# The recurrence branch of a hybrid encoder layer: products that read PSUM, first taps on ScalarE, gates as plain float32

## The chip, the cores and the metric

The kernel runs on one NeuronCore of a Trainium2 chip. The core has five engines with a queue each: TensorE (PE; its weight loads appear as PEld), VectorE (DVE), ScalarE (ACT), GpSimd (POOL) and SyncE (SP), which here only issues DMAs. Matrix products are written to PSUM; everything else lies in SBUF. The metric is the device time of one execution in microseconds (us). Where a time comes from the trace, it is counted from the first instruction of the profiled execution.

## The reference

One layer of an encoder trunk is computed for 1024 tokens of width 1024 in float32: a mixer of two groups, a cross-attention into 256 memory rows, and a gated MLP with a small convolution. The change lies in group A of the mixer. Cut to that group:

```
h    = rms_norm(x, attn_norm)
proj = h @ w_in                       # 1024 x 1440
xr, yg = proj[..., :512], proj[..., 512:1024]
xf = depthwise_conv(xr, conv_w[0], conv_b[0], 3, 0)    # width 4, causal
xb = depthwise_conv(xr, conv_w[1], conv_b[1], 0, 3)    # width 4, anti-causal
def rg_lru(x, ...):
    r = sigmoid(block_diag(x, w_a) + b_a)              # 8 blocks of 64 x 64
    i = sigmoid(block_diag(x, w_i) + b_i)
    log_a = -8 * r * softplus(-lam);  a = exp(log_a)
    b = sqrt(-expm1(2 * log_a)) * (i * x)
    return scan of h[t] = a[t] * h[t-1] + b[t]         # backwards for xb
lru_out = (rg_lru(xf, ...) + rg_lru(xb, ...)) * gelu(yg)
```

The other 416 columns of `proj` are the latents of group B, an attention of 8 heads.

## The kernel before

Channels lie on the 128 partitions and the 1024 tokens along the free dimension, so the 512 channels of group A are four tiles j = 0..3 (`NJ`), each with two directions d. The normalised input stands transposed in SBUF as two halves: `hT[h][0]` is rounded to float32r, `hT[h][1]` is what the rounding left out. Every large product is made of three products of such halves (`mm3`, lines 110 to 113: high by high, high by low, low by high); weights are split into `whi` and `wlo` by `wsplit` (lines 124 to 142), mostly on POOL (lines 133 and 134).

`in_proj` (line 297) makes one 128 x 1024 tile of the projection with 2 x 8 x 3 products of 512 columns in a PSUM tile of pool `pb2`. That pool holds two such tiles, and both the projections and, later, the latents (`pslat`) and the stage behind them take turns in it.

`xr_stage` (line 340) copies the projection into SBUF on ACT (line 345), between three zero columns on either side (lines 343, 344). The copy frees the PSUM tile. `y_stage` (line 348) does the same for the GeLU branch (line 351) and then forms y * (1 + tanh(c * (y + 0.044715 y^3))) with three products on DVE (lines 353, 354, 356) around a tanh on ACT (line 355).

`lru_stage` (line 358) does the two directions of one tile. For each direction: the first tap with the bias on POOL (line 365), three more taps on DVE (line 367); the split of the result, `xh` on ACT (line 370) and `xl` on DVE (line 371); the gates as 4 x 3 products into four PSUM tiles `psg` of 512 columns (the call at line 379; every product is issued by the helper at line 108); tanh, exp, tanh and square root on ACT (lines 385 to 390, which switch between two activation tables, so that each direction loads a table twice); then on DVE `m` (line 392) and `thi` (line 393), on POOL their product (line 394), and on DVE the scan (lines 397, 399). The two directions are added on POOL (line 401), and line 403 multiplies the sum with the GeLU branch on DVE.

The gate weights of two tiles at a time come from `gate_unit` (line 314): eight DMAs into a zeroed staging tile `raw` (pool `wp`, two of them, shared with all weight loads), then split into `whi` and `wlo` (two of the twelve `w` tiles). In lines 508 to 525 the stages are called in this order: the first two projections and gate weights, the rotary tables, then for each tile its GeLU branch, its recurrence and the projection of a later tile; behind the last tile come the latents (line 417), eight of them, one for each 128 tokens. Behind those come the query, key and value products (`pq`, `pk`).

Instructions are not issued in the order of the program. The framework that builds the kernel orders each engine's queue beforehand, by the order of the program and by when it expects operands and buffers to be ready; it puts in all waits, also those for a buffer's release. On the chip each queue then runs in that fixed order. Tiles with one tag share its buffers: `xf` and `xr` have two each, `th0` two, `th1` four.

Of the kernel before, what the change touches and what calls it, by code (L numbers as in the profile page):

```python
# [11 lines left out]
F32 = mybir.dt.float32  # L12
# [7 lines left out]
S = 1024  # L20
# [63 lines left out]
def trunk_layer(ctx: ExitStack, tc: tile.TileContext, a: dict, out: bass.AP):  # L84
# [35 lines left out]
    def wunit(load, n=1024, gains=None, eng="pool"):  # L120
        raw = wload(load)
        return wsplit(raw, n, gains, eng)
# [34 lines left out]

# [1 line left out]
    bcs = ExitStack()  # L159
# [17 lines left out]

    # normed x, transposed
    hT = [[big.tile([P, KD, 512], F32R, tag="big", name=f"hT{h}{s}") for s in range(2)] for h in range(2)]
# [21 lines left out]

    # parameter columns
    RR = tp.tile([P, 6, P], F32, tag="xr", bufs=2, name="RR")
# [31 lines left out]
    def col(name, i=0):  # L235
        r = rows[name] + i
        return pcols[:, r:r + 1]
# [28 lines left out]

    # half biases, softplus of -lambda
    hb = const.tile([P, 16], F32, name="hb")
# [45 lines left out]
    def gate_unit(jj):  # L314
        def load(raw):
            pool.memset(raw, 0.0)
            rv = raw.rearrange("p (j d g c) -> p j d g c", j=2, d=2, g=2)
            for b in range(2):
                for gi, nm in enumerate(("lru_w_a", "lru_w_i")):
                    for d in range(2):  # L320
                        nc.sync.dma_start(
                            rv[64 * b:64 * b + 64, :, d, gi, 64 * b:64 * b + 64],
                            a[nm][0, d].rearrange("(j b) p c -> b p j c", b=2)[b][:, 2 * jj:2 * jj + 2, :])
        wg[jj] = wunit(load)

# [13 lines left out]

    def xr_stage(j):  # L340
        ps = in_proj(j * P)
        xr = tp.tile([P, S + 6], F32, tag="xr", bufs=2, name="xr")
        pool.memset(xr[:, 0:3], 0.0)
        pool.memset(xr[:, S + 3:S + 6], 0.0)
        act.activation(xr[:, 3:S + 3], ps, AF.Copy)
        return xr

    def y_stage(j):
        ps = in_proj(LRU + j * P)
        y = lru[:, j, :]  # L350
        act.activation(y, ps, AF.Copy)
        t = tp.tile([P, S], F32, tag="yt", bufs=1, name="yt")
        dve.scalar_tensor_tensor(t, y, 0.044715, y, ALU.mult, ALU.mult)
        dve.scalar_tensor_tensor(t, t, 1.0, y, ALU.add, ALU.mult)
        act.activation(t, t, AF.Tanh, scale=math.sqrt(2.0 / math.pi))
        dve.scalar_tensor_tensor(y, t, 1.0, y, ALU.add, ALU.mult)

    def lru_stage(j, xr):
        hs = []
        for d in range(2):  # L360
            i = d * 4 + j
            xf = tp.tile([P, S], F32, tag="xf", name="xf")
            cw = [col("conv_w", (d * 4 + k) * 4 + j) for k in range(4)]
            o = 3 * d
            pool.tensor_scalar(xf, xr[:, o:o + S], cw[0], col("conv_b", i), ALU.mult, ALU.add)
            for k in range(1, 4):
                dve.scalar_tensor_tensor(xf, xr[:, o + k:o + k + S], cw[k], xf, ALU.mult, ALU.add)
            xh = tp.tile([P, S], F32R, tag="th0", name="xh")
            xl = tp.tile([P, S], F32R, tag="th1", bufs=4, name="xl")
            act.activation(xh, xf, AF.Copy)  # L370
            dve.tensor_sub(xl, xf, f(xh))
            wh, wl = wg[j // 2]
            pss = []
            for h in range(2):
                for g in range(2):
                    ps = pb1.tile([P, 512], F32, tag="b1", name="psg")
                    wo = ((j % 2) * 4 + d * 2 + g) * P
                    sl = slice(h * 512, (h + 1) * 512)
                    mm3(ps, wh[:, wo:wo + P], wl[:, wo:wo + P], xh[:, sl], xl[:, sl], True, True)
                    pss.append(ps)  # L380
            thr = tp.tile([P, S], F32, tag="th0", name="thr")
            thi = tp.tile([P, S], F32, tag="th1", bufs=4, name="thi")
            for h in range(2):
                for g in range(2):
                    act.activation((thr, thi)[g][:, h * 512:(h + 1) * 512], pss[h * 2 + g], AF.Tanh,
                                   bias=hb[:, g * 8 + i:g * 8 + i + 1], scale=0.5)
            av = tp.tile([P, S], F32, tag="a", name="av")
            act.activation(av, thr, AF.Exp, bias=sp4[:, 8 + i:9 + i], scale=sp4[:, 8 + i:9 + i])
            act.activation(thr, thr, AF.Tanh, bias=sp2[:, i:i + 1], scale=sp2[:, i:i + 1])
            act.activation(thr, thr, AF.Sqrt, scale=0.25)  # L390
            m = thr
            dve.scalar_tensor_tensor(m, av, 1.0, thr, ALU.add, ALU.mult)
            dve.scalar_tensor_tensor(thi, thi, 1.0, xf, ALU.add, ALU.mult)
            pool.tensor_mul(thi, thi, m)
            h = thi
            if d == 0:
                dve.tensor_tensor_scan(h, av, thi, 0.0, ALU.mult, ALU.add)
            else:
                dve.tensor_tensor_scan(h[:, ::-1], av[:, ::-1], thi[:, ::-1], 0.0, ALU.mult, ALU.add)
            hs.append(h)  # L400
        pool.tensor_add(hs[0], hs[0], hs[1])
        y = lru[:, j, :]
        dve.scalar_tensor_tensor(y, hs[0], 0.5, y, ALU.mult, ALU.mult)

    # latents, q, k, v
    wl_ = []
# [29 lines left out]
    def rotated(dst, src, tmp, i, t0, n, nh):  # L436
        # dst [P, n, nh, 32]: the rows src of token tiles t0.., rotated, times their gains
        C = rC[i][:, t0:t0 + n, :].unsqueeze(2).to_broadcast([P, n, nh, ROPE])
        for a_, b_ in ((0, HALF), (HALF, 0)):
            Sb = rS[i][:, t0:t0 + n, a_:a_ + HALF].unsqueeze(2).to_broadcast([P, n, nh, HALF])  # L440
            pool.tensor_tensor(tmp[:, :, :, a_:a_ + HALF], src[:, :, :, b_:b_ + HALF], Sb, ALU.mult)
        pool.tensor_tensor(dst, src, C, ALU.mult)
        pool.tensor_add(dst, dst, tmp)
# [96 lines left out]
    def inv_root(r, tmp):  # L540
        # r -> r ** -0.5 by Newton steps from a guess out of the exponent
        y, b = tmp
        dve.tensor_scalar(y.bitcast(I32), r.bitcast(I32), 1, None, ALU.logical_shift_right)
        dve.tensor_scalar(y.bitcast(I32), y.bitcast(I32), -1, 0x5f3759df, ALU.mult, ALU.add)
        for k in range(3):
            dve.tensor_tensor(b, r, y, ALU.mult)
            dve.scalar_tensor_tensor(b, b, -0.5, y, ALU.mult, ALU.mult)
            dve.scalar_tensor_tensor(y if k < 2 else r, b, 1.5, y, ALU.add, ALU.mult)

    def head_stats(p, th, tmp):  # L550
        # rotates the queries of a head pair, token tiles th * 4 ..; sums of squares of its queries and keys
        if th == 0:
# [24 lines left out]
    def squares(key, src, first, acc, tmp, last=False):  # L577
        # running sum of squares over the channel tiles of a group
        if first:
            sacc[key] = acc([P, S], "acc")  # L580
            act.activation(sacc[key], src, AF.Square)
        else:
            t = tmp([P, S], "acct")
            act.activation(t, src, AF.Square)
            if last:
                dve.tensor_add(sacc[key], sacc[key], t)
                return
            for c in chunks():
                pool.tensor_add(sacc[key][:, c], sacc[key][:, c], t[:, c])
# [3 lines left out]

    # keys and values of the memory
    mT = [[wp.tile([P, 4, MEM], F32R, tag="w", name="mT") for _ in range(2)]
# [80 lines left out]

# [1 line left out]
    cs = ExitStack()  # L678
# [98 lines left out]
    def values(u, part):  # L777
        # part 0 / 1: the two halves of the keys of query pair u
        H, qq = divmod(u, NT // 2)
# [73 lines left out]

# [1 line left out]
    xp = ctx.enter_context(tc.tile_pool(name="xp", bufs=NT, side="right", reuse_waits="tile"))  # L855
# [48 lines left out]
    def turned(xs, dst, o):  # L904
        # xs [P, D] transposed into dst(q) = (hi, lo) [P, 4, ...] at columns o..
        for q in range(2):
# [10 lines left out]
    def headnorm(ps):  # L917
        # rms-norm of the heads of ps [P, 512], without gains
        s4 = dp.tile([P, MH], F32, tag="s4", bufs=2, name="s4")
# [196 lines left out]

# [1 line left out]
    fs = ExitStack()  # L1118
# [96 lines left out]
```

## Time and profile before

| what | value |
|---|---|
| device time, three runs | 1489.05, 1489.11, 1490.06 us (median 1489.11) |
| span of the profiled execution | 1487.0 us, 17902 instructions |
| the profiled execution's own time beside its span | not listed apart; the median of the runs lies 2.1 us above the span |
| PE busy | 1408.4 us (95%) |
| DVE, ACT, POOL busy | 905.4 (61%), 547.8 (37%), 631.1 us (42%) |
| PE busy in the 190 us from 40 to 230 | 152.4 us, at a mean granted clock of 0.89 |

The profile is one execution. "Busy" is the time in which an engine worked on an instruction; a row of the groups gives the line, engine, operation, the tiles written and read, the shapes, the count, then the sum and the mean (ns) of the durations and the idle time of the engine just before them. In the page's strip of 40 slices one slice is 37 us and each digit is a busy share in tenths. Matrix products overlap in their pipeline, so the durations of neighbouring products overlap, and their cost is read from one start to the next. A wait is put down to the engine whose signal came last.

The recurrence branch lies between 40 and 230 us. From 320 us on PE is busy 1146 of 1167 us.

### The profile page before, as it was taken

Reading aid. Unit: us, or ns where it says so; the run is one execution under the profiler, and the core shown is the slowest. Engines: PE = TensorE matmul, PEld = TensorE weight load, DVE = VectorE, ACT = ScalarE, POOL = GpSimd, SP = SyncE. Lnnn points to the kernel's source line nnn. Section 1 sums busy time; section 2 is a strip of 40 time slices with the busy share of each in tenths; the row PEclk is TensorE's granted clock in tenths of the full one; section 3 lists DMA queues with packets and bytes.
Section 4 is the critical chain, followed back from the end, with each engine's and each line's share of the span. In section 5 each row is a group of like instructions: output and inputs, shape, how many; then the busy total and the mean of one; then the engine's idle time right before and its main releaser. Section 6 shows DMA issues by size and latency. Waiting matters only on the chain.

```text
span 1487.0 us, 17902 instructions
## 1 busy us (share of the span) xinstructions
PE 1408.4 (95%) x6996; PEld 1186.8 (80%) x6996; DVE 905.4 (61%) x1260; ACT 547.8 (37%) x904; POOL 631.1 (42%) x612
## 2 busy tenths in 40 slices
PE   6888678998999999999999999999999999999998
PEld 5766578787889888888888888888888888888887
DVE  5879887799999855576645434435343444534335
ACT  5255674688888842355322110101111020111110
POOL 7768686456786811010334142322314232231310
PEclk9989889999999999999999999999999999999999
DMA  5211011200000052101112020211102021110102
GB/s 182 64 38 34 25 43 29 100 1 1 1 1 1 1 172 84 57 2 29 43 29 85 29 71 29 66 47 43 57 29 71 29 59 55 43 57 29 57 0 113
DMA packets 72036, 70.92 MB, mean 48 GB/s; under 512 B 4859, under 2 KB 59408, under 8 KB 71952
## 3 DMA queue, kind: packets, MB, share of 16 engines
q1 hardware_dynamic: 71951, 69.78, 15.1%
q8 instruction: 55, 0.90, 0.2%
q14 instruction: 30, 0.24, 0.1%
HBM read 65.58 MB, written 4.19 MB: 47 GB/s over the span
## 4 chain that ended last, share of the span: by engine, by line
PE 71%; DVE 8%; ACT 3%; POOL 2%; issue 1%; DMA 0%; ACTq 0%; DVEq 0%; POOLq 0%; SPq 0%
PE psup L108 32%; PE psdn L108 16%; PE psP L108 6%; PE psq L108 3%; PE psS L108 3%; PE psmo L108 3%; PE po L108 2%; DVE st L752 2%; DVE pT L775 2%; PE psT L771 2%; PE pq L108 1%; ACT pr L756 1%; PE psn L910 1%; PE psMS L108 1%; PE pmo L108 1%
## 5 line engine op out<-in xcount | busy, mean ns | idle before, releaser
L108 PE MATMUL psup<-h,whi 128*128 128x512 f32 x1408 | 437.5, 389 | 1.1 <-DVE gu L1143 0.9
L108 PEld LDWEIGHTS psup<-h,whi 128*128 128x128 f32 x1408 | 264.2, 188 | 56.8 <-issue 1.2
L133 POOL TENSOR_SCALAR whi<-raw 128x1024 fp32r<-128x1024 f32 (+2 forms) x82 | 91.1, 1111 | 447.3 <-PE psup L108 239.8
L108 PE MATMUL psup<-h,wlo 128*128 128x512 f32 x704 | 273.9, 389 | 0.0
L1142 DVE SCALAR_TENSOR_TENSOR gu<-psup,fcw,gu 128x1023 f32<-128x1023 f32 x44 | 56.4, 1283 | 251.3 <-ACT gu L1141 251.3
L1141 ACT ACTIVATE gu<-psup,fcw 128x1024 f32<-128x1024 f32 x44 | 53.2, 1209 | 421.9 <-PE psup L108 421.9
L134 POOL TENSOR_TENSOR wlo<-raw,whi 128x1024 fp32r<-128x1024 f32 (+2 forms) x82 | 203.2, 2478 | 6.2
L1172 DVE TENSOR_TENSOR x<-x,psdn 128x512 f32<-128x512 f32 x176 | 119.3, 685 | 104.0 <-PE psdn L108 103.3
L108 PEld LDWEIGHTS psup<-h,wlo 128*128 128x128 f32 x704 | 132.1, 188 | 27.4
L108 PE MATMUL psdn<-wlo,ah 128*128 128x512 f32 x336 | 130.7, 389 | 0.0
L108 PE MATMUL psdn<-whi,al 128*128 128x512 f32 x336 | 130.7, 389 | 0.0
L108 PE MATMUL psdn<-whi,ah 128*128 128x512 f32 x336 | 130.5, 389 | 0.1
L108 PE MATMUL psS<-kT,qT 96*128 96x512 f32 x384 | 103.9, 404 | 5.3 <-ACT pr L756 5.2
L758 POOL TENSOR_SCALAR pr<-pr,st 128x1024 f32<-128x1024 f32 x64 | 72.0, 1125 | 53.6 <-DVE st L757 32.1
L108 PE MATMUL psin<-hT,whi 128*128 128x512 f32 (+1 forms) x288 | 87.4, 386 | 1.1 <-ACT hT L199 1.0
L775 DVE TENSOR_TENSOR pT<-psT,pT 128x512 fp32r<-128x512 f32 x128 | 84.5, 679 | 6.2 <-ACT pT L774 6.1
L756 ACT ACTIVATE pr<-psS,st,rqk 128x1024 f32<-128x1024 f32 x64 | 77.2, 1207 | 18.2 <-DVE st L754 14.0
L108 PEld LDWEIGHTS psS<-kT,qT 96*128 96x128 f32 x384 | 67.5, 189 | 19.3 <-ACT pr L756 8.1
L752 DVE TENSOR_REDUCE st<-psS 128x1 f32<-128x1024 f32 x64 | 77.7, 1214 | 8.0 <-PE psS L108 8.0
L108 PE MATMUL po<-pT,vt 128*128 128x256 f32 x512 | 72.2, 287 | 3.6 <-DVE pT L775 3.3
L108 PEld LDWEIGHTS psdn<-whi,ah 128*128 128x128 f32 x336 | 63.1, 188 | 13.5 <-DVE x L1172 0.5
L771 PE MATMUL psT<-ident,pr 128*128 128x128 f32 x512 | 68.3, 273 | 5.7 <-POOL pr L758 3.7
(307 smaller groups left out, 2651.7 us busy)
## 6 DMA issues: line engine op xcount, KB each, us to landing
raw<-in_w_up SPq DMA_DIRECT2D x44, 512.0 KB
raw<-in_w_down SPq DMA_DIRECT2D x22, 512.0 KB
xt<-in_x SPq DMA_DIRECT2D x8, 512.0 KB
raw<-in_w_in SPq DMA_DIRECT2D x8, 512.0 KB
raw<-in_w_mem_kv SPq DMA_DIRECT2D x8, 512.0 KB
raw<-in_w_out SPq DMA_DIRECT2D x8, 512.0 KB
x<-in_x SPq DMA_DIRECT2D x8, 512.0 KB
out<-x SPq DMA_DIRECT2D x7, 512.0 KB
```

The source lines that it names most:

```text
L108: return pe.matmul(ps, lhsT=l, rhs=r, start=start, stop=stop)
L133: pool.tensor_scalar(hi[:, sl], raw[:, sl], 1.0, 0.0, ALU.mult, ALU.add)
L134: pool.tensor_sub(lo[:, sl], raw[:, sl], f(hi)[:, sl])
L752: dve.tensor_reduce(st[:, 0:1], psS, AX.X, ALU.max, negate=True)
L756: act.activation(pr, psS, AF.Exp, bias=st[:, 1:2], scale=r, accum_out=st[:, 2:3])
L758: scaled[s] = pool.tensor_scalar(pr, pr, st[:, 3:4], 0.0, ALU.mult, ALU.add)
L771: pe.transpose(ps[:, i * P:(i + 1) * P], pr[:, (n * 4 + i) * P:(n * 4 + i + 1) * P], ident)
L775: dve.tensor_sub(pTs[s // 2][n][1][:, :, qi * P:(qi + 1) * P], pv, f(dh))
L910: pe.transpose(ps[:, k * P:(k + 1) * P], xs[:, kk * P:(kk + 1) * P], ident)
L1141: act.activation(g, ps, AF.Identity, bias=fcv[:, 3, jj:jj + 1], scale=fcv[:, 1, jj:jj + 1])
L1142: dve.scalar_tensor_tensor(g[:, 1:], ps[:, :S - 1], fcv[:, 0, jj:jj + 1], g[:, 1:], ALU.mult, ALU.add)
L1172: dve.tensor_add(xs, xs, ps)
```

## The change

The change touches `gate_unit`, `xr_stage`, `y_stage` and `lru_stage`; elsewhere only comment lines are blanked.

- The projection of the x-branch is no longer copied to SBUF. Two Identity activations on ACT (one for each direction) read the PSUM tile and write the first tap with the bias; they write all 1024 columns, so no zero columns are needed. The six other taps, on DVE, read the projection in PSUM, and each leaves out the columns that would fall outside. The taps stand in `xr_stage`, thus ahead of the recurrence of the tiles before. Their two results use the tag `xf` for even tiles and `xr` for odd ones.
- The GeLU branch is not copied either. ACT squares it out of PSUM, and the two remaining DVE products read it there.
- The gates are one product of plain float32 operands in place of three of float32r halves: no `xh` and `xl`, no split of the gate weights, which are loaded into one `w` tile without a staging tile.
- The sum of the two directions moves from POOL to DVE, and so does the product of line 394 for the last tile.

```diff
     def gate_unit(jj):
-        def load(raw):
-            pool.memset(raw, 0.0)
-            rv = raw.rearrange("p (j d g c) -> p j d g c", j=2, d=2, g=2)
...
-        wg[jj] = wunit(load)
+
+        w = wp.tile([P, 1024], F32, tag="w", name="wgate")
+        pool.memset(w, 0.0)
+        rv = w.rearrange("p (j d g c) -> p j d g c", j=2, d=2, g=2)
...
+        wg[jj] = w
...
     def xr_stage(j):
+
         ps = in_proj(j * P)
-        xr = tp.tile([P, S + 6], F32, tag="xr", bufs=2, name="xr")
-        pool.memset(xr[:, 0:3], 0.0)
-        pool.memset(xr[:, S + 3:S + 6], 0.0)
-        act.activation(xr[:, 3:S + 3], ps, AF.Copy)
-        return xr
+        xfs = [tp.tile([P, S], F32, tag=("xf", "xr")[j % 2], bufs=2, name="xf") for _ in range(2)]
+        cw = [[col("conv_w", (d * 4 + k) * 4 + j) for k in range(4)] for d in range(2)]
+        for d in range(2):
+            act.activation(xfs[d], ps, AF.Identity, bias=col("conv_b", d * 4 + j), scale=cw[d][3 - 3 * d])
+        for n in range(1, 4):
+            dve.scalar_tensor_tensor(xfs[0][:, n:], ps[:, :S - n], cw[0][3 - n], xfs[0][:, n:], ALU.mult, ALU.add)
+        for n in range(1, 4):
+            dve.scalar_tensor_tensor(xfs[1][:, :S - n], ps[:, n:], cw[1][n], xfs[1][:, :S - n], ALU.mult, ALU.add)
+        return xfs
 
     def y_stage(j):
         ps = in_proj(LRU + j * P)
         y = lru[:, j, :]
-        act.activation(y, ps, AF.Copy)
         t = tp.tile([P, S], F32, tag="yt", bufs=1, name="yt")
-        dve.scalar_tensor_tensor(t, y, 0.044715, y, ALU.mult, ALU.mult)
-        dve.scalar_tensor_tensor(t, t, 1.0, y, ALU.add, ALU.mult)
+        act.activation(t, ps, AF.Square, scale=math.sqrt(0.044715))
+        dve.scalar_tensor_tensor(t, t, 1.0, ps, ALU.add, ALU.mult)
         act.activation(t, t, AF.Tanh, scale=math.sqrt(2.0 / math.pi))
-        dve.scalar_tensor_tensor(y, t, 1.0, y, ALU.add, ALU.mult)
-
-    def lru_stage(j, xr):
+        dve.scalar_tensor_tensor(y, t, 1.0, ps, ALU.add, ALU.mult)
+
+    def lru_stage(j, xfs):
         hs = []
         for d in range(2):
             i = d * 4 + j
-            xf = tp.tile([P, S], F32, tag="xf", name="xf")
-            cw = [col("conv_w", (d * 4 + k) * 4 + j) for k in range(4)]
-            o = 3 * d
-            pool.tensor_scalar(xf, xr[:, o:o + S], cw[0], col("conv_b", i), ALU.mult, ALU.add)
-            for k in range(1, 4):
-                dve.scalar_tensor_tensor(xf, xr[:, o + k:o + k + S], cw[k], xf, ALU.mult, ALU.add)
-            xh = tp.tile([P, S], F32R, tag="th0", name="xh")
-            xl = tp.tile([P, S], F32R, tag="th1", bufs=4, name="xl")
-            act.activation(xh, xf, AF.Copy)
-            dve.tensor_sub(xl, xf, f(xh))
-            wh, wl = wg[j // 2]
+            xf = xfs[d]
             pss = []
             for h in range(2):
                 for g in range(2):
                     ps = pb1.tile([P, 512], F32, tag="b1", name="psg")
                     wo = ((j % 2) * 4 + d * 2 + g) * P
                     sl = slice(h * 512, (h + 1) * 512)
-                    mm3(ps, wh[:, wo:wo + P], wl[:, wo:wo + P], xh[:, sl], xl[:, sl], True, True)
+                    mm(ps, wg[j // 2][:, wo:wo + P], xf[:, sl], True, True)
                     pss.append(ps)
...
-            pool.tensor_mul(thi, thi, m)
+            (dve if j == NJ - 1 else pool).tensor_mul(thi, thi, m)
...
-        pool.tensor_add(hs[0], hs[0], hs[1])
+        dve.tensor_add(hs[0], hs[0], hs[1])
         y = lru[:, j, :]
         dve.scalar_tensor_tensor(y, hs[0], 0.5, y, ALU.mult, ALU.mult)
```

More of the change, by code (lines that the diff above doesn't have):

```diff
@@ L314, in gate_unit @@
     def gate_unit(jj):
-        def load(raw):
-            pool.memset(raw, 0.0)
-            rv = raw.rearrange("p (j d g c) -> p j d g c", j=2, d=2, g=2)
[L318 to L323, printed above, removed]
-        wg[jj] = wunit(load)
+        w = wp.tile([P, 1024], F32, tag="w", name="wgate")
+        pool.memset(w, 0.0)
+        rv = w.rearrange("p (j d g c) -> p j d g c", j=2, d=2, g=2)
+        for b in range(2):
+            for gi, nm in enumerate(("lru_w_a", "lru_w_i")):
+                for d in range(2):
+                    nc.sync.dma_start(
+                        rv[64 * b:64 * b + 64, :, d, gi, 64 * b:64 * b + 64],
+                        a[nm][0, d].rearrange("(j b) p c -> b p j c", b=2)[b][:, 2 * jj:2 * jj + 2, :])
+        wg[jj] = w
     ssl = const.tile([P, NT], F32, name="ssl")
@@ L341, in xr_stage @@
         ps = in_proj(j * P)
-        xr = tp.tile([P, S + 6], F32, tag="xr", bufs=2, name="xr")
-        pool.memset(xr[:, 0:3], 0.0)
-        pool.memset(xr[:, S + 3:S + 6], 0.0)
-        act.activation(xr[:, 3:S + 3], ps, AF.Copy)
-        return xr
+        xfs = [tp.tile([P, S], F32, tag=("xf", "xr")[j % 2], bufs=2, name="xf") for _ in range(2)]
+        cw = [[col("conv_w", (d * 4 + k) * 4 + j) for k in range(4)] for d in range(2)]
+        for d in range(2):
+            act.activation(xfs[d], ps, AF.Identity, bias=col("conv_b", d * 4 + j), scale=cw[d][3 - 3 * d])
[4 more added lines that the diff above has]
+        return xfs
     def y_stage(j):
```

## The prediction

> **What bounds the kernel now.** I read the engines' busy time by stretches first, then who waited for whom, then the groups of each engine.
>
> ```profile
> PEclk9989889999999999999999999999999999999999
> 40.00:230.00 190.00, 152.36 (x645) 126.88 (x645) 163.99 (x137) 105.90 (x147) 144.84 (x106) 0.89 0.13 37
> 230.00:320.00 90.00, 82.13 (x452) 70.90 (x453) 73.34 (x168) 53.31 (x112) 48.29 (x67) 1.00 0.16 53
> ```
>
> The columns of the last two rows are the length, then busy time of PE, PEld, DVE, ACT and POOL, granted clock, DMA share and GB/s. The branch is the stretch from 40 to 230 us, and only there is the clock granted to PE below full. DVE is the busiest engine in it, 164.0 of 190 us; behind it PE leads again. What is saved in the branch moves all that follows, as long as nothing later waits for its own data.
>
> ```profile
> PE psg L108 <- DVE xl L371: 22.5, 5, 6.3
> PE psg L108 <- ACT xh L370: 13.5, 5, 5.2
> ACT yt L355 <- DVE yt L354: 11.9, 3, 7.5
> ```
>
> These are the waits: total, times, longest. PE stood 22.5 + 13.5 = 36.0 us before gate products, all for the two halves of the convolved tile. Both come last in a chain of taps, split and subtraction through DVE.
>
> ```profile
> 42.48 0.40 PE L108 MATMUL psin<-hT,whi 128*128 128x512 f32 x1
> 102.83 0.63 PE L108 MATMUL psg<-xh,wlo 128*128 128x512 f32 x1
> 103.26 0.63 PE L108 MATMUL psg<-xh,whi 128*128 128x512 f32 x1
> 130.88 0.61 PE L108 MATMUL psin<-hT,whi 128*128 128x512 f32 x2
> 131.56 0.39 PE L108 MATMUL psin<-hT,whi 128*128 128x512 f32 x1
> 226.63 0.35 PE L108 MATMUL pslat<-wlo,hT 128*128 128x416 f32 x1
> 226.82 0.35 PE L108 MATMUL pslat<-whi,hT 128*128 128x416 f32 x1
> ```
>
> PE's own need: between 130.88 and 131.56 start three products of 512 columns (two in the row, one left out), so 0.227 us each; a latent product takes 0.19. After the wait ahead of 102.83 the pace is 0.43, the half clock. Seven projections from 42.48 on are 7 x 48 x 0.227 = 76.3, the gates 96 x 0.227 = 21.8, the latents 8 x 24 x 0.19 = 36.5: 134.6 us. The last latent product ends at 227.2, so 184.7 passed and 50 were lost: 36 to waits, most of the rest to the slow clock behind them. So the branch is a DVE queue that PE waits on.
>
> ```profile
> L367 DVE SCALAR_TENSOR_TENSOR xf<-xr,pcols,xf 128x1024 f32<-128x1024 f32 x24 | 42.1, 1761 | 8.1 <-POOL xf L365 8.0
> L393 DVE SCALAR_TENSOR_TENSOR thi<-thi,xf 128x1024 f32<-128x1024 f32 x8 | 15.7, 1963 | 0.0
> L397 DVE TENSOR_TENSOR_SCAN thi<-av,thi 128x1024 f32<-128x1024 f32 x4 | 12.7, 3167 | 2.3 <-POOL thi L394 2.3
> L354 DVE SCALAR_TENSOR_TENSOR yt<-yt,lru 128x1024 f32<-128x1024 f32 x4 | 10.4, 2602 | 0.0
> L371 DVE TENSOR_TENSOR xl<-xf,xh 128x1024 fp32r<-128x1024 f32 x8 | 10.4, 1300 | 0.0
> L399 DVE TENSOR_TENSOR_SCAN thi<-av,thi 128x1024 f32<-128x1024 f32 x4 | 9.8, 2451 | 1.0 <-POOL thi L394 1.0
> L392 DVE SCALAR_TENSOR_TENSOR thr<-av,thr 128x1024 f32<-128x1024 f32 x8 | 9.7, 1216 | 0.8 <-ACT thr L390 0.8
> L353 DVE SCALAR_TENSOR_TENSOR yt<-lru 128x1024 f32<-128x1024 f32 x4 | 7.6, 1909 | 0.0
> L403 DVE SCALAR_TENSOR_TENSOR lru<-thi,lru 128x1024 f32<-128x1024 f32 x4 | 5.5, 1382 | 2.3 <-POOL thi L401 2.3
> L356 DVE SCALAR_TENSOR_TENSOR lru<-yt,lru 128x1024 f32<-128x1024 f32 x4 | 4.8, 1210 | 1.2 <-ACT yt L355 1.2
> ```
>
> Ten groups make up 128.7 of DVE's 164.0 us. The same form takes 1.21 us in one line and 1.76 to 2.60 on the mean in others. Two places show why:
>
> ```profile
> 144.66 4.61 DVE L367 SCALAR_TENSOR_TENSOR xf<-xr,pcols,xf 128x1024 f32<-128x1024 f32 x2
> 144.81 3.37 POOL L394 TENSOR_TENSOR thi<-thi,thr 128x1024 f32<-128x1024 f32 x1 [2.29 <-DVE thr L392]
> 798.35 2.41 POOL L134 TENSOR_TENSOR wlo<-raw,whi 128x1024 fp32r<-128x1024 f32 x1
> 798.62 1.28 DVE L1142 SCALAR_TENSOR_TENSOR gu<-psup,fcw,gu 128x1023 f32<-128x1023 f32 x1 [3.57 <-ACT gu L1141]
> ```
>
> With both operands in SBUF, DVE and POOL stretch each other (two taps 4.61 us, the product 3.37). With one operand in PSUM the same operation runs in 1.28 inside a POOL instruction, and neither is stretched.
>
> **The change part by part.** The MLP behind holds the added forms:
>
> ```profile
> L1142 DVE SCALAR_TENSOR_TENSOR gu<-psup,fcw,gu 128x1023 f32<-128x1023 f32 x44 | 56.4, 1283 | 251.3 <-ACT gu L1141 251.3
> L1141 ACT ACTIVATE gu<-psup,fcw 128x1024 f32<-128x1024 f32 x44 | 53.2, 1209 | 421.9 <-PE psup L108 421.9
> L370 ACT ACTIVATE xh<-xf 128x1024 fp32r<-128x1024 f32 x8 | 8.5, 1062 | 28.6 <-DVE xf L367 26.5 <-POOL thi L394 2.0
> L345 ACT ACTIVATE xr<-psin 128x1024 f32<-128x1024 f32 x4 | 4.1, 1018 | 8.2 <-POOL RR L276 7.7 <-POOL RR L291 0.4
> L351 ACT ACTIVATE lru<-psin 128x1024 f32<-128x1024 f32 x4 | 4.1, 1013 | 1.7 <-PE psin L108 1.7
> ```
>
> DVE: 24 taps out of PSUM x 1.283 = 30.8; two GeLU products x 4 x 1.283 = 10.3; L392 stays 9.7; `xl` and L353 go. With all that remains unstretched: L393 8 x 1.216 = 9.7, scans 8 x 2.451 = 19.6, L403 4.9, the sums now on DVE 4 x 1.216 = 4.9, the last tile's products 2 x 1.216 = 2.4; together 92.3. With the stretch as measured (L393 15.7, scans 22.5, L403 5.5, sums 4 x 1.963 = 7.9, products 3.9): 106.3. DVE loses 22.4 to 36.4 us, 29 in the middle.
>
> [...]
>
> ACT: off 8.5 + 4.1 + 4.1; on 8 Identities x 1.209 = 9.7 and 4 squares x 1.06 (as L370) = 4.2: 2.8 less of 106 busy in 190, with no bearing on the end. The DVE taps wait for these Identities, which wait for a buffer that line 393 of two tiles earlier frees; queued behind them on ACT are the tanhs of gates.
>
> ```profile
> L394 POOL TENSOR_TENSOR thi<-thi,thr 128x1024 f32<-128x1024 f32 x8 | 25.0, 3125 | 16.8 <-DVE thr L392 16.7
> L365 POOL TENSOR_SCALAR xf<-xr,pcols 128x1024 f32<-128x1024 f32 x8 | 17.5, 2185 | 10.2 <-DVE thi L393 10.2
> L401 POOL TENSOR_TENSOR thi<-thi 128x1024 f32<-128x1024 f32 x4 | 11.9, 2968 | 0.0
> ```
>
> POOL: 17.5 + 11.9 + a quarter of 25.0 = 35.6 us off, besides the gate splits; it leaves 109 of 145, and fewer encounters with DVE. The weights' staging tile comes free for projection loads; their DMAs stay on SP, covered, since no wait of PE was for a projection's weights.
>
> PE: per gate one plain float32 product of 512 columns for three. The nearest row:
>
> ```profile
> L336 PE MATMUL pss<-ones,acc 128*128 128x2 f32 x32 | 3.7, 243 | 0.0
> ```
>
> It is plain float32 but two columns wide and gives no rate. Bounds: one pass, 0.227 us; or four partial products of halves (the split form leaves out low by low) at the half clock, 4 x 0.427 = 1.71. I take four at full clock, 0.91: 32 x 0.91 = 29.1 against 21.8, 7.3 more. [...] PE's need becomes 141.9; from 42.48 the latents could end at 184.4, 42.8 earlier.
>
> What is late next: a PSUM tile was free after a copy of 1.02. Now an x-tile is held 2 x 1.209 + 6 x 1.283 = 10.1 us, a GeLU tile 1.06 + 1.283 + 1.06 + 1.283 = 4.7. Filling the other takes 48 x 0.227 = 10.9, so 10.1 just hides; with a scan and an L393 between the taps (about 5) it doesn't, though gates can run meanwhile. I charge 4 us in all.
>
> Sum: DVE's 29 less 4 is 25. Check: a branch of 165 has PE at 142, a loss of 23 where 50 was. The span of 1487.0 becomes 1462.0; with the 2.1 us between it and the median, 1464.
>
> **The rivals.**
> *Clean* (0.10): the taps are done early, the stretch vanishes, gates wait for nothing, PE is the bound. The full 42.8 us: 1446. Against it: DVE would still need 126 to 140 of 148 us.
> *Held tiles* (0.12): four fills (first GeLU tile, x-tiles 2 and 3, last GeLU tile) wait for an x-tile's release. If each hold grows by the longest wait above (7.5), a scan (3.17) and an L393 (1.96) to 22.7, PE stands 11.8 us four times, 47 in place of the 4: 25 gained less 43 is 18 slower, 1507. It turns slower when a hold passes 18.2 us, a stall of 7.3. [...]
> *Dear float32* (0.10): 1.71 each is 54.7, or 25.6 over my sum: no gain, 1489.
> *No effect at the end* (0.06): the stage behind waits for its own weights and the gain stays in the branch: 1489. PE's 82 of 90 us there speaks against it.
>
> **How the numbers follow.** My forecast has 0.62, with a gain of 12 to 38. The range reaches down to the clean case, 1446, and up to 1483, a gain of 6, which takes in half-held tiles and a float32 product between my price and the upper bound. About 0.2% (3 us) is what a measurement can tell from no change. Faster: forecast 0.62, clean 0.10, and 0.09 in which held tiles (0.03) or dear float32 (0.06) take only part of the gain: 0.81. Same: no effect 0.06 and 0.01 of dear float32: 0.07. Slower: the other 0.09 of held tiles and 0.03 of dear float32 with some stalls on top: 0.12.
>
> **What would show it.** Waits of PE's `psg` near zero instead of 36; taps at 1.28 without spread; `psg` starts 0.91 apart; latents ending near 202. Wrong, if `psin` or `pslat` waits for DVE (held tiles), if `psg` starts lie over 1.2 apart, or if the latents end early and the end does not move.

## The result and the profile after

| | before | after |
|---|---|---|
| device time, median (lowest to highest) | 1489.59 (1489.05 to 1493.52), 4 runs | 1465.92 us (1464.37 to 1470.66), 4 runs |
| profiled execution | span 1487.0 us | span 1462.3 us, its time 1464.37 |
| last latent product starts | 226.82 us | 205.55 us |

The ratio is 0.984, with a 95% interval of 0.9818 to 0.9863: 23.7 us less. The forecast was 1464, with 1446 to 1483 around it.

The busy time by stretches, profile after; columns as in the prediction's first fence:

```profile
40.00:230.00 190.00, 170.88 (x747) 136.18 (x746) 141.24 (x176) 114.77 (x173) 101.53 (x109) 0.96 0.15 43
230.00:320.00 90.00, 85.46 (x497) 74.22 (x496) 77.90 (x165) 63.12 (x121) 44.48 (x58) 0.98 0.13 42
```

PE now leads in the branch's stretch, 170.9 of 190 us where it had 152.4, and the clock went from 0.89 to 0.96. The stretch is no longer the branch alone: the latents end at about 205.9, and 24 us of the next stage lie in it.

PE's waits from 40 to 215 us (total, times, longest; the row left out belongs to the next stage):

```profile
PE psin L108 <- DVE xf L351: 6.6, 2, 5.2
PE pslat L108 <- ACT pslat L425: 5.8, 1, 5.8
PE psg L108 <- POOL RR L286: 4.7, 1, 4.7
PE psg L108 <- ACT thr L380: 1.1, 1, 1.1
...
PE psg L108 <- ACT thi L380: 0.2, 1, 0.2
```

The 36.0 us for the convolved tile's halves are gone. The gates wait 4.7 + 1.1 + 0.2 = 6.0; new are two waits for a PSUM tile that the taps still read (6.6) and one for a latent's tile that ACT still reads (5.8). The 4.7 are put down to an operation of POOL on `RR`, a tile that no gate reads. The third tap of the first x-tile ended at 53.53 and the first gate product started at 53.74; in the third profile of the change the two stand at 56.53 and 56.74, the same 0.21 apart. So what this gate waits for is most likely DVE's tap.

DVE's groups from 40 to 205 us, in the order of the list (a row of the rotary tables is left out):

```profile
L349 DVE SCALAR_TENSOR_TENSOR xf<-psin,pcols,xf 128x1023 f32<-128x1023 f32 (+2 forms) x12 | 15.3, 1276 | 0.2
L351 DVE SCALAR_TENSOR_TENSOR xf<-psin,pcols,xf 128x1023 f32<-128x1023 f32 (+2 forms) x12 | 15.3, 1276 | 0.1
L388 DVE SCALAR_TENSOR_TENSOR thi<-thi,xf 128x1024 f32<-128x1024 f32 x8 | 11.4, 1430 | 1.9 <-ACT thi L380 1.9
L387 DVE SCALAR_TENSOR_TENSOR thr<-av,thr 128x1024 f32<-128x1024 f32 x8 | 11.4, 1426 | 11.6 <-ACT thr L385 11.6
L394 DVE TENSOR_TENSOR_SCAN thi<-av,thi 128x1024 f32<-128x1024 f32 x4 | 10.8, 2695 | 3.9 <-POOL thi L389 3.9
L392 DVE TENSOR_TENSOR_SCAN thi<-av,thi 128x1024 f32<-128x1024 f32 x4 | 9.8, 2455 | 2.5 <-POOL thi L389 2.5
L396 DVE TENSOR_TENSOR thi<-thi 128x1024 f32<-128x1024 f32 x4 | 8.5, 2126 | 0.1
L398 DVE SCALAR_TENSOR_TENSOR lru<-thi,lru 128x1024 f32<-128x1024 f32 x4 | 8.0, 1996 | 0.0
...
L359 DVE SCALAR_TENSOR_TENSOR yt<-yt,psin 128x1024 f32<-128x1024 f32 x4 | 4.8, 1211 | 0.0
L361 DVE SCALAR_TENSOR_TENSOR lru<-yt,psin 128x1024 f32<-128x1024 f32 x4 | 4.8, 1206 | 2.3 <-ACT yt L360 2.3
```

These sum to 100.1 us, to which the last tile's two products (L389) add 2 x 1.225: 102.6, where before had 128.7. What reads PSUM is flat (taps of 1.267 to 1.283 us, GeLU products of 1.21 on the mean); what has both operands in SBUF is still stretched where it meets POOL, above all the sum (L396) and L398 with their mean of 2.0 to 2.1 us against 1.2.

The gates on PE, by start:

```profile
152.70 3.59 PE L108 MATMUL psg<-xf,wgate 128*128 128x512 f32 x8
155.73 0.75 PE L108 MATMUL pslat<-whi,hT 128*128 128x416 f32 x1
156.32 0.35 PE L108 MATMUL pslat<-wlo,hT 128*128 128x416 f32 x1
```

The row x8 is four products: each of the 32 plain float32 products leaves two records, 64 in all. The record of the latent product behind them starts at 155.73, inside that row, and is 0.75 us long, where the next one has 0.35; so the time is read up to that next start, 156.32. Less 0.19 for the latent product between, four products took 3.43 us, 0.86 each, at a granted clock of 1.00.

### The profile page after: what moved, and what is told of

Same layout as the page of the kernel before. It is cut to its first block, busy times and chain, and to the rows that moved or that the text cites. A ratio compares the mean times of both kernels' runs of the same rounds, so it can differ in the third digit from the quotient of the medians.

```text
span 1462.3 us, 17808 instructions
## 1 busy us (share of the span) xinstructions
PE 1405.3 (96%) x6964; PEld 1176.7 (80%) x6964; DVE 866.1 (59%) x1254; ACT 545.8 (37%) x900; POOL 570.4 (39%) x586
## 4 chain that ended last, share of the span: by engine, by line
PE 78%; DVE 9%; ACT 7%; POOL 3%; issue 2%; DMA 1%; SPq 0%; ACTq 0%; DVEq 0%; POOLq 0%
PE psup L108 33%; PE psdn L108 16%; PE psP L108 6%; PE psS L108 3%; PE psq L108 3%; PE po L108 3%; PE psmo L108 3%; PE pslat L108 2%; PE psT L766 2%; DVE st L747 2%; PE psin L108 2%; DVE pT L770 2%; PE pq L108 1%; PE pkv L108 1%; POOL wlo L134 1%
## 5 line engine op out<-in xcount | busy, mean ns | idle before, releaser
L134 POOL TENSOR_TENSOR wlo<-raw,whi 128x1024 fp32r<-128x1024 f32 (+2 forms) x80 | 195.3, 2441 | 11.4 <-PE psin L108 5.4
L751 ACT ACTIVATE pr<-psS,st,rqk 128x1024 f32<-128x1024 f32 x64 | 77.2, 1207 | 17.4 <-DVE st L749 13.4
L769 ACT ACTIVATE pT<-psT 128x512 fp32r<-128x512 f32 x128 | 71.0, 596 | 8.1 <-PE psT L766 7.6
```

The costliest lines, as they stand in the source:

```text
L134: pool.tensor_sub(lo[:, sl], raw[:, sl], f(hi)[:, sl])
L751: act.activation(pr, psS, AF.Exp, bias=st[:, 1:2], scale=r, accum_out=st[:, 2:3])
L769: act.activation(dh, pv, AF.Copy)
```

## The experiments

The theory going in was the prediction's: DVE's queue is what PE waits for, so time follows the work taken off DVE. Against it stood that the hold of the PSUM tiles decides, that one part alone carries the gain, and that PE has become the bound. All medians are of five rounds; ratios are to the kernel before on the same chip. "Last latent" is the start of the branch's last product in the profiled execution, which stood at 226.8 before and at 205.6 in the profile above.

| kernel | median us | ratio, interval | last latent |
|---|---|---|---|
| gates alone | 1486.36 | 0.9975 (0.9956 to 0.9993) | 224.8 |
| split gates back | 1474.26 | 0.9883 (0.9858 to 0.9908) | 212.0 |
| both copies back | 1483.48 | 0.9946 (0.9926 to 0.9965) | 219.4 |
| GeLU copy back | 1467.13 | 0.9846 (0.9822 to 0.987) | 210.9 |
| x copy back, one buffer | 1479.69 | 0.9924 (0.9899 to 0.995) | 219.8 |
| x copy back, two buffers | 1478.33 | 0.9915 (0.9896 to 0.9934) | 216.8 |
| sums on POOL | 1467.12 | 0.984 (0.9813 to 0.9868) | 209.5 |
| sum later | 1469.1 | 0.9853 (0.9831 to 0.9875) | 209.9 |
| gates issued twice | 1481.97 | 0.9938 (0.9914 to 0.9962) | 219.2 |
| 24 more reductions on DVE | 1474.21 | 0.9881 (0.9857 to 0.9905) | 212.2 |
| the change, second time | 1467.91 | 0.9856 (0.983 to 0.9882) | 207.7 |
| the change, third time | 1468.54 | 0.9851 (0.983 to 0.9871) | 209.7 |

The ratios of the change itself, 0.984, 0.9856 and 0.9851, and its last latents, 205.6, 207.7 and 209.7, show how far one kernel differs from itself: most intervals reach some 4 us to either side, and a single profile's last latent moves by as much.

**Gates alone.** The kernel before, with only the gates as plain float32 (and their weights loaded without a split); taps, copies and sums as before.

```diff
-            xh = tp.tile([P, S], F32R, tag="th0", name="xh")
-            xl = tp.tile([P, S], F32R, tag="th1", bufs=4, name="xl")
-            act.activation(xh, xf, AF.Copy)
-            dve.tensor_sub(xl, xf, f(xh))
...
-                    mm3(ps, wh[:, wo:wo + P], wl[:, wo:wo + P], xh[:, sl], xl[:, sl], True, True)
+                    mm(ps, wg[j // 2][:, wo:wo + P], xf[:, sl], True, True)
```

> The kernel before with the plain float32 gates alone; the projection is still copied to SBUF. Theory A (DVE's load is what counts, shared between the split that goes and the stretch that ends): xl takes 10.4 of the 26 us that DVE loses between the two profiles, so about 0.4 of the 24.7 us between the two spans, 9 to 12 us less than before. Theory B (the chain counts: all 36 us of PE's waits were for the two halves, so without them the gates are ready): 18 to 25 us less than before. Theory C (the gain is all from operands in PSUM): 0 to 4 us less.

Measured: 0.9975, some 3.7 us of gain; of the three expectations only that of operands in PSUM (0 to 4) has it. Its stretch from 40 to 230 us, ACT's longest wait, PE's four longest, and its largest DVE group:

```profile
40.00:230.00 190.00, 154.55 (x634) 118.75 (x633) 149.72 (x139) 98.41 (x139) 133.40 (x111) 0.91 0.13 40
```
```profile
ACT yt L356 <- DVE yt L355: 38.3, 3, 15.1
...
PE psg L108 <- DVE xf L368: 14.1, 4, 7.1
PE psg L108 <- issue: 8.6, 1, 8.6
PE pslat L108 <- ACT pslat L426: 6.2, 1, 6.2
PE psg L108 <- ACT thr L381: 6.0, 1, 6.0
```
```profile
L368 DVE SCALAR_TENSOR_TENSOR xf<-xr,pcols,xf 128x1024 f32<-128x1024 f32 x24 | 46.4, 1939 | 6.4 <-POOL xf L366 6.2
```

DVE is busy 149.7 us where it was 164.0, so 14.3 us of DVE work went, although the taps took more (46.4 us in place of 42.1), and about a quarter of it shows in the time. PE's four rows say why: the waits for the two halves are gone, but 14.1 + 8.6 + 6.2 + 6.0 = 34.9 us of others stand where 36.0 had stood. ACT's tanh of the GeLU branch waited 38.3 us for DVE's product ahead of it, where it had waited 11.9. Time does not follow DVE's load one to one.

**Split gates back.** The change, with the edit above undone (`xh`, `xl`, the weights' split and three products for each gate).

> The changed kernel with the gates put back to three products of split halves; convolution and GeLU still read PSUM, and the sums stay on DVE. Theory A: 12 to 15 us less than before. Theory B: 0 to 6 us less, since xh and xl are back between the taps and the gates. Theory C: 20 to 25 us less.

Measured: 0.9883, a gain of 17.4 us, between the expectations of DVE's load (12 to 15) and of operands in PSUM (20 to 25); the chain through the halves (0 to 6) is out. So the plain float32 gates are worth 3.7 us by themselves and 4 to 6 on top of the rest (by which of the change's three ratios one takes; the intervals overlap), although they cost PE 27.5 - 21.8 = 5.7 us more. PE's largest wait here:

```profile
PE psin L108 <- DVE xf L350: 19.7, 2, 14.5
```

The x-tile's hold grows: 19.7 us of waits for it in place of 6.6. Before the longer one, the second x-tile's first tap starts at 76.41, where the change has 65.30. Two `xl` of 1.21 us stand ahead of it in DVE's queue, but also operations of the rotary tables, several of which take 1.2 to 2.5 us in place of 0.3, so `xl` alone doesn't account for it. That is the held-tile wait as the prediction described it, at one fill with more (14.5) than the 11.8 us that the rival charged for each of four, and the kernel is still far ahead of before.

**Both copies back.** The change, with both projections copied to SBUF by ACT again (x into the GeLU tile of the last j, which isn't needed yet).

```diff
-        ps = in_proj(j * P)
+        pp = in_proj(j * P)
+        ps = lru[:, NJ - 1, :]
+        act.activation(ps, pp, AF.Copy)
...
-        ps = in_proj(LRU + j * P)
+        pp = in_proj(LRU + j * P)
...
+        ps = y
+        act.activation(y, pp, AF.Copy)
```

> The changed kernel with one ACT copy of each projection into SBUF put back (the x-branch into the still unused fourth tile of lru, the GeLU branch into its own tile); the Identity taps, the DVE taps and the GeLU products read the copy, in the same places as in the change. Theory A: DVE's operations with both operands in SBUF are stretched by POOL again, 24 taps and 8 GeLU products at up to 0.5 us each, so 5 to 12 us slower than the change. Held tiles as the main limit left: the PSUM tile is free after 1.0 us, so PE's 6.6 us of waits for taps go and it is 2 to 6 us faster than the change. If neither matters: within 2 us of the change.

Measured: 0.9946, 13 to 16 us behind the change, by which of its three ratios one takes; the expectation by stretched operands had 5 to 12 and that by held tiles the other sign. PE's two largest waits:

```profile
PE psg L108 <- ACT thr L384: 19.7, 4, 11.4
PE pslat L108 <- ACT pslat L429: 12.2, 1, 12.2
```

The waits of `psin` are gone, as a theory of held tiles wants it, and the kernel is slower: in their place stand these, both behind ACT. Most of the change's gain hangs on reading PSUM, not on the moved taps and Identities, which all remain here. (The order of ACT's queue changed too; see the x copy below.)

**GeLU copy back alone.** The second half of that diff.

> The change, with the copy of the GeLU branch's projection to SBUF back (one ACT copy of about 1.02 us for each of four tiles; the square and the two products then read SBUF), the x-branch still read in PSUM. Both copies together cost 16 to 17 us. Theory A, what counts is that operations with both operands in SBUF are stretched by POOL and stand in a chain: the eight GeLU products of 4 of the chains then cost a third of the whole, 3 to 7 us over the change (1469 to 1473). Theory H, holding a PSUM tile costs: a GeLU tile is let go 4 to 8 us earlier, the two psin waits behind the Square (8.6 and less) shrink, and the time falls by 3 to 6 us (1460 to 1463).

Measured: 0.9846, the same as the change on the same chip (0.9851). The `psin` waits went, but one `pslat` wait grew:

```profile
PE pslat L108 <- ACT pslat L427: 10.8, 1, 10.8
PE psg L108 <- issue: 6.2, 1, 6.2
PE psg L108 <- ACT thr L382: 4.3, 2, 2.5
```

6.6 us of `psin` went and 5.0 of `pslat` and 3.2 of the tanh's came. Both numeric expectations missed; this half of the change is worth nothing that these runs can tell.

**x copy back alone**, the first half of the diff, in one buffer and then, in a run of its own, in two (`lru[:, NJ - 1 - j % 2, :]`).

> The change, with the copy of the x-branch's projection to SBUF back (into the GeLU tile of the last j, which isn't needed yet: one ACT copy for each of four tiles, and since it is one buffer a copy also waits for the taps of the tile before), the GeLU branch still read in PSUM. Theory A: 24 taps are stretched by POOL from 1.28 to 1.6 to 1.8 us and the copy stands ahead of them, so most of the 16 to 17 us of both copies comes from here, 9 to 14 us over the change (1475 to 1480). Theory H: the x-tile's hold falls from over 10 to about 1 us, the psin waits (6.6) go, and the time falls by 3 to 7 us (1459 to 1463).

> As the run with only the x-branch copied (+11 us over the change), but the copies take turns in two SBUF tiles in place of one; the queues of PE, ACT, POOL and SyncE are then the same as in that run, instruction for instruction. There the second copy waited 16.0 us on ACT for the taps of the first tile. If that single buffer made the loss, the time falls to the change's, 1464 to 1470 (ratio 0.983 to 0.986). If the loss comes from taps that are stretched with both operands in SBUF, and from the scans, products and GeLU step queued behind them, little changes: 1475 to 1482 (ratio 0.990 to 0.994), and the wait of the gates for ACT's tanh, 18.6 us there, stays over 12.

Measured: 11 us behind the change on the same chip with one buffer (0.9924), and 0.9915 with two; that the copy stood in one buffer is thus not what costs. Both results lie where taps stretched in SBUF were expected to put them (9 to 14 us, and 0.990 to 0.994). Half of the taps with two buffers, as minimum, median and maximum in ns, beside the same half of the change's; the other halves are alike (3367 and 1282 at most):

```profile
L351 DVE SCALAR_TENSOR_TENSOR xf<-lru,pcols,xf x12: 1269/1286/3407, 48.1 to 146.6; 128x1023 f32<-128x1023 f32 x4, 128x1022 f32<-128x1022 f32 x4, 128x1021 f32<-128x1021 f32 x4
```
```profile
L349 DVE SCALAR_TENSOR_TENSOR xf<-psin,pcols,xf x12: 1267/1279/1283, 48.0 to 132.3; 128x1023 f32<-128x1023 f32 x4, 128x1022 f32<-128x1022 f32 x4, 128x1021 f32<-128x1021 f32 x4
```

At its shortest, a tap takes the same 1.27 us from SBUF and from PSUM. Beside POOL it takes up to 3.4 from SBUF, and from PSUM never over 1.283. (The two longest taps started inside a POOL instruction that reads SBUF, and ended 1.08 and 1.09 us behind its end: 51.50 to 54.91 beside 50.41 to 53.83, and 59.74 to 63.11 beside 58.62 to 62.02. In the profile after, two operations of DVE with both operands in SBUF do the same, each 1.08 us behind: the sum, 94.22 to 97.46, beside POOL's L389, 92.07 to 96.38, and L398, 100.28 to 103.21, beside POOL's L134, 98.30 to 102.13.) By the groups of DVE the 24 taps sum to 21.2 + 20.0 = 41.2 us, against 30.6.

How that reaches PE is seen where it stalls longest, in the run with two buffers; DVE, ACT and PE by start:

```profile
131.36 4.04 DVE L396 TENSOR_TENSOR_SCAN thi<-av,thi 128x1024 f32<-128x1024 f32 x1 [2.48 <-POOL thi L391]
...
138.92 2.95 DVE L400 SCALAR_TENSOR_TENSOR lru<-thi,lru 128x1024 f32<-128x1024 f32 x1
...
148.98 1.21 DVE L361 SCALAR_TENSOR_TENSOR yt<-yt,psin 128x1024 f32<-128x1024 f32 x1
```
```profile
150.22 1.06 ACT L362 ACTIVATE yt<-yt 128x1024 f32<-128x1024 f32 x1 [15.78 <-DVE yt L361]
151.18 0.67 ACT L382 ACTIVATE thr<-psg,hb 128x512 f32<-128x512 f32 x1
```
```profile
151.90 2.07 PE L108 MATMUL psg<-xf,wgate 128*128 128x512 f32 x2 [13.76 <-ACT thr L382]
```

PE waits 13.76 us for a bank that ACT's tanh of a gate frees. That tanh stands in ACT's queue behind the GeLU tanh, which waits 15.78 us for a DVE product; and that product stands in DVE's queue behind a scan, the sum, L400 and six taps, several of them stretched. In the change, the same product (L359) started at 137.31, and the GeLU tanh behind it did not wait. Not all of the 9 to 12 us is the stretch, though: in this passage the scan, the sum, L400 and the taps took some 6 us more than their shortest, and DVE came to it already late, the scan starting at 131.36 where the change's stood at 122.77. ACT's order in this passage is the change's (Identities, Square, two tanhs of gates, the GeLU tanh), but ahead of it the framework ordered ACT's queue otherwise in these kernels: for the first GeLU tile the Square stands two steps earlier, and for the second a copy and a tanh of the gates stand ahead of the Identities and the Square. How the cost divides between stretch and order is open; no run held the order and changed only the place of the operands.

**Sums on POOL.** The sum of the directions and the last tile's product back on POOL.

```diff
-            (dve if j == NJ - 1 else pool).tensor_mul(thi, thi, m)
+            pool.tensor_mul(thi, thi, m)
...
-        dve.tensor_add(hs[0], hs[0], hs[1])
+        pool.tensor_add(hs[0], hs[0], hs[1])
```

> The changed kernel with the sum of the two directions and the last tile's product back on POOL. Theory A: DVE has 11.0 us less to do, POOL about 15 more with two operands in SBUF; the two nearly cancel, within 3 us of the change. If POOL's load were the bound: 5 to 10 us slower than the change. If DVE is still the bound: 5 to 8 us faster.

Measured: 0.984, as the change and as expected for loads that nearly cancel. Moving the sums (8.5 us) and the last products (2.5) from DVE to POOL makes no difference that these runs can tell; that DVE's load is still the bound (5 to 8 us faster) is not borne out.

**Sum later.** The sum and the product behind it called after the taps of the later projection, for tiles 0 and 1 (`lru_stage` returns a function `combine`, which is called behind `xr_stage`).

> The changed kernel with the sum of the two directions and the product of tiles 0 and 1 called after the projection of the later tile in place of before it, so that the six taps which hold its PSUM tile come ahead of them in DVE's queue. If held tiles are what PE still waits for (5.2 us before 111.01): 3 to 6 us faster than the change. If another wait takes its place: within 2 us of the change.

Measured: 0.9853, no difference; and the experiment tested nothing. On DVE the sum still ran ahead of the taps:

```profile
98.11 3.24 DVE L398 TENSOR_TENSOR thi<-thi 128x1024 f32<-128x1024 f32 x1
...
107.02 3.90 DVE L349 SCALAR_TENSOR_TENSOR xf<-psin,pcols,xf 128x1023 f32<-128x1023 f32 x3
```

The framework orders the queue, and the changed order of the program did not move these instructions behind the taps. What a shorter hold at this place would bring was not tried.

**Gates issued twice.** Each gate product a second time into the same bank, with the same values.

```diff
                     mm(ps, wg[j // 2][:, wo:wo + P], xf[:, sl], True, True)
+                    mm(ps, wg[j // 2][:, wo:wo + P], xf[:, sl], True, True)
```

> The changed kernel with each of the 32 gate products issued twice into the same PSUM tile, the second overwriting the first, so the values are the same. Between 152.70 and 155.73 us of the changed profile four of them start in about 0.86 us each, so this adds 27.5 us to PE's need in the branch. If PE is close to the bound there (141 of 162 us needed): 15 to 25 us slower than the change. If the chain through ACT and DVE is the bound and PE fills gaps: 3 to 10 us slower.

Measured: 1481.97, 14 us over the change on the same chip by the medians and 12 by the ratios, between the two expectations (15 to 25, 3 to 10), for 32 x 0.86 = 27.5 us of PE work. About half of what is added to PE shows in the time.

**24 more reductions on DVE.** Three reductions of `av`, to a tile that nothing reads, ahead of `m` in each direction.

```diff
+            for _ in range(3):
+                dmy = sm.tile([P, 1], F32, tag="dmy", bufs=4, name="dmy")
+                dve.tensor_reduce(dmy, av, AX.X, ALU.max)
```

> The changed kernel with three extra reductions on DVE for each direction (maximum of av, 128x1024 to 128x1, the results unused), 24 in all at about 1.2 us, so 29 us more for DVE with one SBUF operand each. If DVE's load is still the bound: 18 to 28 us slower than the change. If DVE now has slack (123 us busy of 162): 5 to 15 us slower, by the 3.6 us that lie in the chain of each direction where the next tile waits for it.

Measured: 1474.21, 6.3 us over the change on the same chip by the medians and 3.7 by the ratios, whose intervals overlap, for

```profile
L388 DVE TENSOR_REDUCE dmy<-av 128x1 f32<-128x1024 f32 x24 | 27.8, 1207 | 4.0 <-ACT av L383 4.0
```

27.8 us of DVE work. Under a quarter shows, so the expectation of a bound DVE (18 to 28) is out. DVE's waits say where part of the rest went, first in this kernel, then in the change:

```profile
DVE cns L431 <- POOL s L430: 12.3, 7, 7.2
...
DVE thr L390 <- ACT thr L385: 0.3, 2, 0.2
```
```profile
DVE cns L428 <- POOL s L427: 18.1, 6, 7.3
DVE thr L387 <- ACT thr L385: 11.6, 6, 3.5
```

Ahead of `m` 11.3 us of idle time went and 4.0 ahead of the reductions came, and 5.8 went ahead of the latents' scaling: about 13 us of the work lie where DVE had stood idle. After the change DVE is no longer the bound; PE's work costs more of its length than DVE's does.

**The change again**, twice.

> The changed kernel once more, for the comparison on the same chip: a ratio of 0.984 to the kernel before, within its interval of 0.982 to 0.986.

> The change itself, beside the two on the same chip: 1464 to 1468 by every theory.

Measured: 1467.91 and 1468.54, ratios of 0.9856 and 0.9851; the second median lies half a microsecond over the expected 1464 to 1468. What lies between single executions of this one kernel is told in the last section.

## Why the prediction was right, and where it was not

- **The bound before.** That PE stood behind a chain through DVE was right: the 36.0 us of waits for the convolved tile's halves went with the change. That this chain is a queue whose load sets the time was too simple. The gates-alone kernel took 14.3 us off DVE and gained 3.7; 27.8 us put on DVE after the change cost 4 to 6.
- **The taps.** "24 taps out of PSUM x 1.283" was right: 30.6 us, and no tap outside 1.267 to 1.283. Copying the x-branch to SBUF first makes the kernel 9 to 12 us slower.
- **DVE's sum.** 102.6 us, within 92.3 to 106.3; 26.1 lost where 29 was the middle.
- **Plain float32.** 0.86 us in place of the estimated 0.91, so 27.5 for all; the rival with 1.71 is out. No run shows the four products at 0.227 us of which the 0.91 was made up; they were the author's estimate. The trace shows what one product costs, 6% less than that, and not how it is made.
- **Held tiles.** The sign that was to show the forecast wrong, `psin` waiting for DVE, did appear: 6.6 us, beside the 4 charged for it. The mechanism was real, and its condition was even met once: the third x-tile was held from the Identity's start to its last tap's end,

```profile
91.55 2.30 ACT L347 ACTIVATE xf<-psin,pcols 128x1024 f32<-128x1024 f32 x2 [0.81 <-PE psin L108]
...
106.95 3.91 DVE L351 SCALAR_TENSOR_TENSOR xf<-psin,pcols,xf 128x1023 f32<-128x1023 f32 x3
```
```profile
111.01 1.19 PE L108 MATMUL psin<-hT,whi 128*128 128x512 f32 x2 [5.19 <-DVE xf L351]
```

  19.3 us, over the 18.2 at which the change was to turn slower. It stalled PE 5.19 us and not 8.4, since four gate products of 3.4 us ran in between; and it did so at one of four fills, with 1.4 at another. The rival needed all four. Nor does a shorter hold pay of itself: in the kernels that copy first the waits come back as `pslat` and `psg` (12.2 and 19.7 us with both copies).
- **PE's floor and the end of the branch.** From the first projection of 512 columns at 43.44 to 205.9 are 162.5 us. PE's need is 141.9 less 32 x 0.05, so 140.3: 22 lost, against the 23 of the prediction's check. The waits above make up 18.4 of them. The other 4 are slow clock behind two of the waits: the first four gate products took 5.4 us in place of 3.4, with a mean granted clock of 0.69 from 53.7 to 59.2, and from 111.01 to 115.57 it is 0.54. The branch ended 21.3 us earlier, not 25, and the forecast of 202 for the latents was missed by nearly 4. (The clean case's 126 to 140 us for DVE doesn't follow from its own rows, which give 164.0 less 36.4 and less 22.4, 128 to 142; no term of the sum hangs on it.)
- **The sum.** 25 was forecast for the span, 24.7 came, but not by the same terms: 21.3 lie in the branch and 3.4 behind it. From the last latent product to the end are 1487.0 - 226.8 = 1260.2 us before and 1256.8 after. That the gain reaches the end was right (the rival without effect is out); that nothing is added behind it was not. From the last latent product to the last query product (`pq`) are 37.2 us before and 34.0 after, so 3.2 of the 3.4 lie there. PE's waits in that stretch, the three longest before and then the only one after:

```profile
PE pk L108 <- POOL wlo L134: 1.2, 1, 1.2
PE psm L610 <- DVE mT L614: 1.2, 1, 1.2
PE pq L108 <- ACT hp L637: 1.0, 1, 1.0
```
```profile
PE psc L615 <- DVE mT L609: 0.7, 1, 0.7
```

  With one more of 0.3, 3.7 us of waits for POOL, DVE and ACT became 0.7; what brought these engines there sooner was not tried. That the sum hit 1464 so closely is in part luck: it took a microsecond for each that DVE loses, where the gates alone and the added reductions show a quarter or less, and it put nothing behind the branch. And 21.3 and 3.4 are those of one profile; in the third one the last latent starts 17.1 us earlier than before, with 3.1 behind it.
- **What the parts are worth**, along one path through the runs: the gates alone 4 us; from there to the kernel with both copies (taps and Identities early, sums moved) another 4; from there to the change, by reading PSUM, 13 to 16. Undone alone, the x-branch's reading is worth 9 to 12 of these and the GeLU branch's nothing that can be told. Whether the two are worth more together than apart lies within the intervals.

## What to carry to other kernels

Don't price a queue by its load: take the wait that ends last in each tile, follow it back through the queues in which its releaser stands, and ask what stands next there. Where two engines stretch each other over SBUF operands, as DVE and POOL did here (taps of 1.27 us took up to 3.4), reading a product where it lies in PSUM can be worth more than an early release of the tile (9 to 12 us for the x-branch here), so long as PE has other products to run meanwhile. And look in the changed kernel's queues whether an edit moved anything before reading its time.

## What the runs showed of the hardware

Executions of the change itself lay from 1464.25 to 1475.94 us. Two of its profiles, from 420 to 440 us, the profile after and then the second one (columns as before; the clock is the third from the right):

```profile
420.00:440.00 20.00, 19.85 (x137) 17.51 (x137) 19.10 (x43) 16.94 (x32) 16.01 (x23) 1.00 0.00 1
```
```profile
420.00:440.00 20.00, 16.98 (x98) 15.16 (x99) 17.14 (x37) 11.87 (x21) 12.00 (x17) 0.83 0.00 1
...
424.00:428.00 4.00, 4.00 (x19) 3.87 (x18) 2.71 (x6) 1.87 (x5) 1.49 (x2) 0.50 0.00 0
```
```profile
422.87 2.26 PE L108 MATMUL po<-pT,vt 128*128 128x256 f32 x9 [4.33 <-DVE pT L770]
```

In the second, PE waits 4.33 us in the attention stage behind the branch, and after it the granted clock stands at 0.50 from 424 to 428 and at 0.95 in the next 4 us; 98 records of products stand in the 20 us in place of 137. In the profile after, the same kind of wait is 0.85, at 416.94, and the clock stays at 1.00 from 400 to 440. The tail behind the last latent product shows it over all profiled executions: about 1257 to 1258 us in the change, its third profile and the kernels with gates alone, split gates, the sum later, both copies or the x copy, and about 1263 in the others (the second profile: 1470.6 - 207.7 = 1262.9). The longest wait of this kind is 4.3 or 4.4 us in those five and at most 1.4 in all the rest, before included (1.1, with 1260.2). Why it is sometimes so long was not found. Some 6 us that an edit in the branch has not made, more than several of the edits above are worth; so the last latent's start was read beside each median.
